# Stacking the high and low parts of the 64 sample tokens in one 128-column stationary operand

## The chip, the core and the metric

The kernel runs on one core of one Trainium2 chip. The metric is the device time of one execution in microseconds (us); the number for a kernel is the median of its runs. Five engines work side by side, each through its own list of instructions in order: TensorE (PE, matrix products; PEld is its load of the stationary operand), VectorE (DVE), ScalarE (ACT), GpSimd (POOL) and SyncE (SP), which here only starts DMA transfers. They wait for each other through semaphores.

## What is computed

The reference is one inference step of a hybrid layer, for 2048 prompt tokens and 64 sample tokens of another stream. Cut to what matters:

```python
h = rms_norm(x, norm_g)                      # x: prompt (2048, 1024), sample (64, 1024)
proj = h @ w_in                              # (1024, 6656), then split in ten column groups
o_hg = hgrn2_chunkwise(silu(hg_q), k_in, hg_i, log_f, s_hg)       # 8 heads, carries a state
o_rt = retention_chunkwise(rope(rt_q), rope(rt_k), rt_v, s_rt)    # 4 heads, carries a state
o_xa = softmax(xa_q @ mem_k.T / sqrt(128)) @ mem_v                # 4 heads, 256 memory tokens
mixed = concat([norm(o_hg) * silu(hg_gate), norm(o_rt) * silu(rt_gate), o_xa * silu(xa_gate)])
y = rms_norm(x + mixed @ w_out, final_norm_g)                     # w_out: (2048, 1024)
```

The operands are float32. To keep the accuracy, the kernel splits every operand of a large product into a high part (rounded to the type that TensorE reads in one pass) and a low part (the rest), and sums three products: high x high, high x low, low x high.

## The kernel before

The 2112 tokens are worked on in two groups (GROUPS): tiles of 512 and 512 tokens, then of 512, 256 and 320. The last tile holds 256 prompt tokens and, as its last subchunk, the 64 sample tokens (DEC). For each group the normed, transposed tokens stand in SBUF as a high and a low buffer (ha, hb). Then come, in this order: the retention gates, the values of the retention (RV, `v_group`), its queries and keys (RQ, `retention`), and for each half of the HGRN heads their values (HI, `v_group` again) and four heads; then the memory attention; at the end, over all tokens, the output projection.

Most projections are column-major (`gemm_col`, L243): weights are stationary and tokens move. RV, RQ and the two HI are token-major (`gemm_tok`, L273): 128 tokens, or the 64 sample tokens, are the stationary operand, and 512 weight columns move past them. One such product has 8 slices of the 1024 inputs, and for each three matmuls (L278): high tokens x high weights, low tokens x high weights, high tokens x low weights. That is 24 matmuls. The output projection (`y_half`, L1091) takes one block of 128 tokens (the last block is the 64 sample tokens) and one half of the 1024 output columns: 16 slices of 128, three matmuls each, so 48 matmuls for a half.

What sets the order: PE's and SP's lists stand as the code is written. Around the big products, tails (transposes, scores, state updates) are put into PE's list by a planner (`task`, `poll`): each has a due time in PE's planned time, which `pe()` counts up with every matmul. ACT, DVE and POOL are ordered by a scheduler by priority. Weights come through three staging buffers (wst), are split by ACT (the cast, L240) and DVE (the difference, L241) into six pairs (whi, wlo); a pair comes free where `w_rel` stands (L282: after every second slice of the last token-major product of a stage), which starts the split of a later slab and then its refill by DMA (L141). In the retention each subchunk loads a table for the rotation (cs, L593, three buffers), rotates (L600 to L606, DVE), then its tail transposes r (L618), copies it (L622 to L626, ACT), forms scores (L635), outputs (L651, L655), norms (L675 to L683) and transposes back (L691). `slot()` gives scratch tiles from one pool of 16.

The output projection loads a block of the mixed rows (mst, 512 KB in two transfers), splits it (L240, L241), adds the product to x (L1103), squares with a sum (L1104), scales (L1119) and stores. The x block stands in abuf or xq by turns. `y_load` of the next block is issued in the middle of a block.

Of the kernel before, what the change touches and what calls it, by code (L numbers as in the profile page):

```python
# [63 lines left out]
def layer_kernel(ctx: ExitStack, tc: tile.TileContext, io: dict):  # L64
# [115 lines left out]
    def allow_alloc(tag):  # L180
        return [t.rearrange("p k n -> p (k n)") for t in h_tile(tag, 512 if tag == "a" else 576)]
# [41 lines left out]
    def small(n, tag):  # L223
        return sm.tile([P, n], F32, tag=tag, name=tag)
# [47 lines left out]

    def gemm_tok(ws, ht, o, L, rel=False):  # L273
        ps = acc()
        n = 0
        for kk in range(KT):
            w = wt[ws[kk // 2]]
            for a, b in ((0, 0), (0, 1), (1, 0)):  # L278
                T.matmul(ps[0:L, :], ht[b][:, kk, o:o + L], w[a][:, kk % 2, :], start=(n == 0), stop=(n == 23))  # L279
                n += 1  # L280
                pe(512 / 2400.0)
            if rel and kk % 2 == 1:  # L282
                w_rel()
            if kk < KT - 1:
                poll()
        return ps
# [72 lines left out]
    def h_split(ht, sts, bcs, nt):  # L359
        for kk in range(KT + 1):  # L360
            if kk < KT:
                st = sts[kk]
                V.scalar_tensor_tensor(out=st, in0=st, scalar=ng[:, kk:kk + 1], in1=bcs[:, 0:nt], op0=ALU.mult, op1=ALU.mult)
                S.copy(ht[0][:, kk, 0:nt], st)
            if kk:
                V.tensor_tensor(out=ht[1][:, kk - 1, 0:nt], in0=sts[kk - 1], in1=ht[0][:, kk - 1, 0:nt].bitcast(F32), op=ALU.subtract)  # L366
            yield kk
# [17 lines left out]
    def h_tile(tag, n):  # L385
        return [hpool.tile([P, KT, n], F32R, tag=f"{tag}{i}", name=f"h{tag}{i}") for i in range(2)]
# [201 lines left out]
    def retention(ws, ht, tok0, nt, vt, R, dtab, last_tile):  # L588
        for c, (o, L) in enumerate(subchunks(tok0, nt)):
            t = tok0 + o  # L590
            ti = t // 128
            ct_ = sm.tile([P, 96], F32, tag="cs", name="cs", bufs=3)
# [4 lines left out]
            ps = gemm_tok(ws, ht, o, L, last_tile and o + L == nt)  # L597
            r = slot()
# [204 lines left out]
    def prep_tile(gi, i, gap, sts=None, tot=None, delay=0):  # L803
        tok0, nt = GROUPS[gi][i]
        if i == 0:
            ht = h_tile("a", 512)
        elif i == 1:
            hmap["b"] = h_tile("b", 576)
            ht = [b_[:, :, 0:nt] for b_ in hmap["b"]]
        else:  # L810
            ht = [b_[:, :, 256:256 + nt] for b_ in hmap["b"]]
        done = [False]
        g = prep_h(ht, [L for _, L in subchunks(tok0, nt)], tok0 // 128, io["xT"][:, tok0:tok0 + nt], sts, tot, delay, gap, done)
        task(None, g, 0)
        hmap[gi, i] = ht
        hdone[gi, i] = done
# [16 lines left out]
    mh = h_tile("b", 576)  # L833
# [65 lines left out]
    h0 = h_tile("a", 512)  # L899
# [57 lines left out]

    def y_load(o, raw):
        L = 128 if o < SEQ else DEC
        src = io["x_prompt"][0, o:o + L] if o < SEQ else io["x_sample"][0]  # L960
        if (o // 128) % 2:
# [5 lines left out]
        for mv in raw:  # L967
            hi, lo = slot(F32R), slot(F32R)
            hv = hi.rearrange("p (k l) -> p k l", k=4)[:, :, 0:L]
            lv = lo.rearrange("p (k l) -> p k l", k=4)[:, :, 0:L]  # L970
            split(hv, lv, mv)
            m.append((hv, lv))
# [4 lines left out]
    for gi, tiles in enumerate(GROUPS):  # L977
        hts = [h_get(gi, 0)]

        def v_group(c0):  # L980
            ws = w_get(4)
            out = []
            for (tok0, nt), ht in zip(tiles, hts):
                vs = []
                for o, L in subchunks(tok0, nt):
                    ps = gemm_tok(ws, ht, o, L, tok0 + o + L == tiles[-1][0] + tiles[-1][1])
                    v = vpool.tile([P, 512], F32, tag="v", name="v")
                    S.copy(v[0:L], ps[0:L])
# [102 lines left out]
    def y_half(mx, x, ss, L, half):  # L1091
        ps = acc()
        n = 0
        for kk in range(16):
            w = wo[half, kk]
            m = mx[kk // 4]
            for a, b in ((0, 0), (1, 0), (0, 1)):
                T.matmul(ps[0:L], m[a][:, kk % 4], w[b], start=(n == 0), stop=(n == 47))  # L1098
# [3 lines left out]
        xs = x[half][0:L]  # L1102
        V.tensor_tensor(out=xs, in0=xs, in1=ps[0:L], op=ALU.add)  # L1103
        S.activation(ps[0:L], xs, AF.Square, accum_out=ss[0:L, half:half + 1])  # L1104

    for o in range(0, NTOK, 128):
# [5 lines left out]
        if o + 128 < NTOK:  # L1112
            nxt = y_load(o + 128, mix_fetch(o + 128, 128 if o + 128 < SEQ else DEC, False))
# [106 lines left out]
```

## Time and profile before

| | |
|---|---|
| median of 3 runs | 1980.01 us (1978.01 to 1980.36) |
| span of the profiled execution, first to last instruction | 1976.5 us; the page gives no time of this execution beside its span |
| PE busy | 1936.0 us, 98% of the span |
| DVE, ACT, POOL busy | 1045.4 us (53%), 583.5 us (30%), 161.4 us (8%) |
| mean granted TensorE clock | 0.993 of the full clock |
| DMA | 153.20 MB, 25.3% of the 16 engines' span on the main queue |
| chain that ended last | PE 86%, DVE 6%, DMA 2%, ACT 2% |

The page has the busy time of each engine, the span in 40 slices, the chain of work that ended last and the costliest groups. Below it, the trace can be asked for the instructions in order of time (the timeline), for one line's instructions, and for the waits.

### The profile page before, as it was taken

How to read it: one execution, taken by the hardware profiler on the slowest of the kernel's cores; microseconds unless marked ns; L12 is line 12 of the kernel's file. 1: busy time of each engine (PE TensorE's matmuls, PEld its weight loads, DVE VectorE, ACT ScalarE, POOL GpSimd, SP SyncE). 2: the span in 40 equal slices, each digit the busy share in tenths (PEclk: the TensorE clock that was granted, in tenths of full speed). 3: DMA queues.
4: the chain of work that ended last, by engine and by line, in shares of the span. 5: the costliest groups of instructions: out<-in, count | busy, mean ns of one | idle time of the engine just before them, and what ended most of it. 6: DMA issues, size and time to landing. Idle time of an engine off the chain costs nothing.

```text
span 1976.5 us, 28228 instructions
## 1 busy us (share of the span) xinstructions
PE 1936.0 (98%) x10970; PEld 1624.4 (82%) x10970; DVE 1045.4 (53%) x2505; ACT 583.5 (30%) x1414; POOL 161.4 (8%) x363
## 2 busy tenths in 40 slices
PE   8899999999999999999999999999999999999998
PEld 7788788888888887978788888888889878888885
DVE  6716637762767557417637774477765632222221
ACT  5522223322233434312322332233333521111110
POOL 3100101000100100000101111021100000000000
PEclk8999999999999999999999999999999999999999
DMA  7422311211112524321311111111122442332221
GB/s 249 139 70 66 87 50 48 59 54 49 44 43 59 155 64 137 92 60 53 86 43 48 48 48 48 43 49 48 59 73 73 125 132 85 99 114 86 86 86 43
DMA packets 116742, 153.20 MB, mean 78 GB/s; under 512 B 13313, under 2 KB 79233, under 8 KB 116609
## 3 DMA queue, kind: packets, MB, share of 16 engines
q1 hardware_dynamic: 116608, 151.41, 25.3%
q8 instruction: 86, 1.41, 0.3%
q14 instruction: 48, 0.39, 0.1%
HBM read 117.69 MB, written 33.69 MB: 77 GB/s over the span
## 4 chain that ended last, share of the span: by engine, by line
PE 86%; DVE 6%; DMA 2%; ACT 2%; issue 1%; POOL 1%; SPq 0%; DVEq 0%; POOLq 0%; ACTq 0%
PE acc L249 38%; PE acc L1098 19%; PE acc L279 16%; PE scb L514 2%; PE ob L523 2%; PE ob L555 1%; PE ob L558 1%; PE acc L783 1%; PE ob L739 1%; DVE wlo L241 1%; PE acc L264 1%; PE tr L507 1%; PE tr L574 1%; POOL rs L237 1%; PE tr L761 1%
## 5 line engine op out<-in xcount | busy, mean ns | idle before, releaser
L249 PE MATMUL acc<-hb,whi 128*128 128x320 f32 (+2 forms) x1728 | 414.5, 330 | 0.4 <-DVE hb L366 0.4
L249 PE MATMUL acc<-ha,whi 128*128 128x512 f32 x1120 | 353.3, 397 | 0.0
L249 PEld LDWEIGHTS acc<-hb,whi 128*128 128x128 f32 x1728 | 289.5, 189 | 24.7 <-issue 4.4
L241 DVE TENSOR_TENSOR wlo<-wst,whi 128x1024 fp32r<-128x1024 f32 x118 | 146.5, 1246 | 277.0 <-ACT whi L240 276.0
L249 PE MATMUL acc<-hb,wlo 128*128 128x320 f32 (+2 forms) x864 | 281.5, 326 | 0.0
L249 PEld LDWEIGHTS acc<-ha,whi 128*128 128x128 f32 x1120 | 203.8, 188 | 42.8 <-issue 2.4
L249 PE MATMUL acc<-ha,wlo 128*128 128x512 f32 x560 | 219.1, 391 | 0.0
L240 ACT CAST whi<-wst 128x1024 fp32r<-128x1024 f32 x118 | 123.6, 1050 | 223.2 <-PE acc L249 171.7
L279 PE MATMUL acc<-whi,hb 128*128 128x512 f32 (+1 forms) x576 | 180.0, 394 | 0.0
L249 PEld LDWEIGHTS acc<-hb,wlo 128*128 128x128 f32 x864 | 163.1, 189 | 11.2
L279 PE MATMUL acc<-whi,ha 128*128 128x512 f32 x512 | 161.0, 396 | 0.0
L1098 PE MATMUL acc<-whi,s 128*128 128x512 f32 (+1 forms) x408 | 128.9, 397 | 1.3 <-ACT s L240 1.0
L249 PEld LDWEIGHTS acc<-ha,wlo 128*128 128x128 f32 x560 | 105.1, 188 | 23.0
L279 PEld LDWEIGHTS acc<-whi,hb 128*128 128x128 f32 (+1 forms) x576 | 103.0, 182 | 25.1 <-issue 1.2
L279 PE MATMUL acc<-wlo,hb 128*128 128x512 f32 (+1 forms) x288 | 112.3, 390 | 0.0
L279 PEld LDWEIGHTS acc<-whi,ha 128*128 128x128 f32 x512 | 93.8, 188 | 19.7 <-issue 1.2
L1098 PE MATMUL acc<-hb,s 128*128 128x512 f32 (+1 forms) x408 | 100.3, 402 | 0.0
L279 PE MATMUL acc<-wlo,ha 128*128 128x512 f32 x256 | 100.0, 391 | 0.0
L1098 PE MATMUL acc<-ha,s 128*128 128x512 f32 (+1 forms) x408 | 98.1, 395 | 0.0
L1098 PEld LDWEIGHTS acc<-hb,s 128*128 128x128 f32 (+1 forms) x408 | 77.0, 189 | 20.3
L241 DVE TENSOR_TENSOR s<-mst,s 128x512 fp32r<-128x512 f32 (+1 forms) x64 | 40.3, 672 | 99.2 <-ACT s L240 99.2
L1098 PEld LDWEIGHTS acc<-whi,s 128*128 128x128 f32 (+1 forms) x408 | 75.0, 184 | 21.5 <-ACT s L240 1.3
(223 smaller groups left out, 2888.0 us busy)
## 6 DMA issues: line engine op xcount, KB each, us to landing
wst<-w_in_t SPq DMA_DIRECT2D x104, 512.0 KB, 4.0
mixT<-s SPq DMA_DIRECT2D x64, 256.0 KB, 4.0
mst<-mixT SPq DMA_DIRECT2D x30, 512.0 KB, 5.9
wst<-w_out_t SPq DMA_DIRECT2D x16, 512.0 KB, 4.0
s<-mixT SPq DMA_DIRECT2D x16, 256.0 KB, 3.0
s<-x_prompt SPq DMA_DIRECT2D x16, 256.0 KB, 4.7
xq<-x_prompt SPq DMA_DIRECT2D x16, 256.0 KB, 4.9
abuf<-x_prompt SPq DMA_DIRECT2D x16, 256.0 KB, 5.8
```

The lines of the kernel that those rows point to most:

```text
L237: G.tensor_tensor(out=out, in0=out, in1=nhalf[0:out.shape[0], 0:n], op=ALU.pow)
L240: S.copy(hi, src)
L241: V.tensor_tensor(out=lo, in0=src, in1=hi.bitcast(F32), op=ALU.subtract)
L249: T.matmul(ps[:, 0:nt], w[a][:, kk, :], ht[b][:, kk, 0:nt], start=(n == 0), stop=(n == 23))
L264: T.matmul(ps[:, 0:nt], w[a][:, kk, :], ht[b][:, kk, 0:nt], start=(kk == 0 and a + b == 0), stop=(kk == KT - 1 and a == 1))
L279: T.matmul(ps[0:L, :], ht[b][:, kk, o:o + L], w[a][:, kk % 2, :], start=(n == 0), stop=(n == 23))
L507: T.transpose(trk[0:L, c * 128:(c + 1) * 128], kch[:, c * 128:c * 128 + L], ident)
L514: T.matmul(scb[32 * e:32 * e + 32, c * 128 + 32 * e:c * 128 + L], K[:, c * 128 + 32 * e:c * 128 + 32 * e + 32], Qe[:, c, E_OFF[e]:E_OFF[e] ...
L523: T.matmul(db[:, c * 128:(c + 1) * 128], kT[0:L, c * 128:(c + 1) * 128], vt[c][0:L], start=True, stop=True)
L555: T.matmul(ob[0:L, c * 128:(c + 1) * 128], A[0:L, c * 128:c * 128 + L], vt[c][0:L], start=True, stop=first)
L558: T.matmul(ob[0:L, c * 128:(c + 1) * 128], qst[:, c * 128:c * 128 + L], st[c][0], start=False, stop=True)
L1098: T.matmul(ps[0:L], m[a][:, kk % 4], w[b], start=(n == 0), stop=(n == 47))
```

## The change

For the 64 sample tokens alone, the high and the low part are put side by side: 64 columns of high, 64 of low, in one stationary operand of 128 columns. One matmul with the high weights then gives high x high in output rows 0 to 63 and low x high in rows 64 to 127; a second one, with the low weights, adds high x low (and low x low in the lower rows). A `fold` adds the two halves of the result: ACT copies rows 64 to 127 to a scratch tile, DVE adds that to rows 0 to 63.

- Token-major: the high buffer hb0 grows from 576 to 640 columns a slice, and one more ACT copy, run once when the last tile is prepared, writes the low part of the sample tokens behind the high part (`hstk`). The sample's product is 16 matmuls in place of 24, four times (RV, RQ, HI twice). For RV and HI the fold writes v in place of ACT's copy; for RQ it writes a scratch tile pf, from which the rotation then reads.
- Output projection: the sample's mixed rows are split straight into the stacked form; a half has 32 matmuls in place of 48, and ACT's copy and a second DVE add follow it. The sample block is moved from last place to the last but one; the last block is now the 128 tokens from 1920.
- The rotation tables (cs) have two buffers in place of three, and so have Te and rT of the HGRN heads.

```diff
     def small(n, tag):
-        return sm.tile([P, n], F32, tag=tag, name=tag)
+        return sm.tile([P, n], F32, tag=tag, name=tag, bufs=2 if n == 32 else 3)
...
+    def fold(dst, ps):
+        t = slot()
+        S.copy(t[0:DEC], ps[DEC:P])
+        V.tensor_tensor(out=dst, in0=ps[0:DEC], in1=t[0:DEC], op=ALU.add)
+
     def gemm_tok(ws, ht, o, L, rel=False):
...
             w = wt[ws[kk // 2]]
+            if L == DEC:
+                for a in range(2):
+                    T.matmul(ps, hstk[0][:, kk, :], w[a][:, kk % 2, :], start=(n == 0), stop=(n == 15))
+                    n += 1
+                    pe(512 / 2400.0)
+                if rel and kk % 2 == 1:
+                    w_rel()
+                if kk < KT - 1:
+                    poll()
+                continue
...
+            if kk == KT and nt == 320:
+                S.copy(hstk[0][:, :, DEC:P], ht[1][:, :, 256:320].bitcast(F32))
             yield kk
...
-        return [hpool.tile([P, KT, n], F32R, tag=f"{tag}{i}", name=f"h{tag}{i}") for i in range(2)]
+    def h_tile(tag):
+        return [hpool.tile([P, KT, n], F32R, tag=f"{tag}{i}", name=f"h{tag}{i}") for i, n in enumerate({"a": (512, 512), "b": (640, 576)}[tag])]
...
-            ct_ = sm.tile([P, 96], F32, tag="cs", name="cs", bufs=3)
+            ct_ = sm.tile([P, 96], F32, tag="cs", name="cs", bufs=2)
...
             ps = gemm_tok(ws, ht, o, L, last_tile and o + L == nt)
+            if L == DEC:
+                pf = slot()
+                fold(pf[0:L], ps)
+                ps = pf
...
+    order = list(range(0, SEQ - P, P)) + [SEQ, SEQ - P]
+
     def y_load(o, raw):
...
-            hi, lo = slot(F32R), slot(F32R)
...
+            hi = slot(F32R).rearrange("p (k l) -> p k l", k=4)
+            if L == DEC:
+                split(hi[:, :, 0:L], hi[:, :, L:P], mv)
+                m.append((hi, hi))
+                continue
...
-                    S.copy(v[0:L], ps[0:L])
+                    if L == DEC:
+                        fold(v[0:L], ps)
+                    else:
+                        S.copy(v, ps)
...
-            for a, b in ((0, 0), (1, 0), (0, 1)):
-                T.matmul(ps[0:L], m[a][:, kk % 4], w[b], start=(n == 0), stop=(n == 47))
+            terms = ((0, 0), (1, 0), (0, 1)) if L == P else ((0, 0), (0, 1))
+            for a, b in terms:
+                T.matmul(ps, m[a][:, kk % 4], w[b], start=(n == 0), stop=(n == 16 * len(terms) - 1))
...
         xs = x[half][0:L]
+        if L == DEC:
+            t = slot()
+            S.copy(t[0:L], ps[L:P])
+            V.tensor_tensor(out=xs, in0=xs, in1=t[0:L], op=ALU.add)
         V.tensor_tensor(out=xs, in0=xs, in1=ps[0:L], op=ALU.add)
...
-    for o in range(0, NTOK, 128):
+    for i_, o in enumerate(order):
```

How the lists of the engines change is seen at three places. In the rows, s is a scratch tile, acc a result of PE, tr a transposed result, scb scores, cs the rotation table, mst the loaded mixed rows; a row is line, operation, output<-inputs and shape. Line numbers of the changed kernel are shifted: its L706 is L683 of the kernel before, L623 to L629 are L600 to L606, L651 is L628, L662 is L639, L716 is L693, L649 is L626, L703 is L680, L1140 and L1141 are L1103 and L1104.

DVE at the end of the retention of the second group, before:

```order
L241 TENSOR_TENSOR wlo<-wst,whi 128x1024 x2
L683 TENSOR_TENSOR s<-s,rs_8081 128x512
L628 TENSOR_TENSOR s<-tr,cst 128x256
L600 TENSOR_TENSOR s<-acc,cs 64x512
L693 TENSOR_TENSOR s<-s,tr 128x512
L604 TENSOR_TENSOR s<-acc,cs 64x8x32
L605 TENSOR_TENSOR s<-acc,cs 64x8x32
L606 TENSOR_TENSOR s<-s 64x512
L608 TENSOR_TENSOR s<-s,cst 64x256
```

The same stretch of DVE's list in the changed kernel:

```order
L241 TENSOR_TENSOR wlo<-wst,whi 128x1024 x2
L706 TENSOR_TENSOR s<-s,rs_8082 128x512
L276 TENSOR_TENSOR s<-acc,s 64x512
L623 TENSOR_TENSOR s<-s,cs 64x512
L627 TENSOR_TENSOR s<-s,cs 64x8x32
L628 TENSOR_TENSOR s<-s,cs 64x8x32
L629 TENSOR_TENSOR s<-s 64x512
L631 TENSOR_TENSOR s<-s,cst 64x256
L651 TENSOR_TENSOR s<-tr,cst 128x256
L662 TENSOR_TENSOR s<-scb,s 128x512
L716 TENSOR_TENSOR s<-s,tr 128x512
```

The fold's add (L276) and the sample's rotation now stand ahead of the two passes L651 and L716 that belong to the subchunks before.

ACT at the same place, before:

```order
L240 CAST whi<-wst 128x1024 x3
L622 COPY q2b_139<-tr 64x2x128
L623 COPY q2b_139<-tr 64x2x128
L240 CAST whi<-wst 128x1024
L680 ACTIVATE s,ss_8075<-s 128x128 x4
L626 COPY s<-tr 128x256
```

ACT there in the changed kernel (q2b takes the two copies of the transposed queries, ss a sum of squares):

```order
L240 CAST whi<-wst 128x1024 x4
L645 COPY q2b_139<-tr 64x2x128
L646 COPY q2b_139<-tr 64x2x128
L703 ACTIVATE s,ss_8076<-s 128x128 x4
L275 COPY s<-acc 64x512
L649 COPY s<-tr 128x256
```

The fourth cast of weights has moved ahead of the query copies, and the fold's copy (L275) stands ahead of the key copy L649, for which the scores on PE wait.

ACT at the end of the output projection, before:

```order
L1104 ACTIVATE acc,ss_16599<-xq 128x512 x2
L240 CAST s<-mst 128x4x64 x4
L1104 ACTIVATE acc,ss_16732<-abuf_109 128x512
L1104 ACTIVATE acc,ss_16732<-abuf_111 128x512
L1104 ACTIVATE acc,ss_16866<-xq 64x512 x2
```

And in the changed kernel:

```order
L240 CAST s<-mst 128x4x64 x4
L1141 ACTIVATE acc,ss_16578<-xq 128x512 x2
L1138 COPY s<-acc 64x512
L240 CAST s<-mst 128x512 x3
L1141 ACTIVATE acc,ss_16707<-abuf_109 64x512
L240 CAST s<-mst 128x512
L1138 COPY s<-acc 64x512
L1141 ACTIVATE acc,ss_16707<-abuf_111 64x512
L1141 ACTIVATE acc,ss_16815<-xq 128x512 x2
```

The sample's casts (128x4x64) now come one block earlier, and the four full casts of the last block stand between the two copies of the sample block.

## Rows read from the trace of the kernel before

**Rows 1.** Page, part 1: busy us (share of the span) and instructions of each engine.

```profile
PE 1936.0 (98%) x10970; PEld 1624.4 (82%) x10970; DVE 1045.4 (53%) x2505; ACT 583.5 (30%) x1414; POOL 161.4 (8%) x363
```

**Rows 2.** Timeline of PE, second HI: start us, us, engine, line, instruction.

```profile
1243.96 0.61 PE L279 MATMUL acc<-whi,hb 128*128 128x512 f32 x2
...
1250.08 0.63 PE L279 MATMUL acc<-whi,hb 128*64 128x512 f32 x2
...
1255.60 0.61 PE L249 MATMUL acc<-ha,whi 128*128 128x512 f32 x2
```

**Rows 3.** Timeline of DVE, last two blocks of the output projection.

```profile
1935.38 0.69 DVE L1103 TENSOR_TENSOR abuf<-abuf,acc 128x512 f32<-128x512 f32 x1 [0.38 <-PE acc L1098]
1946.59 0.69 DVE L1103 TENSOR_TENSOR abuf<-abuf,acc 128x512 f32<-128x512 f32 x1 [10.52 <-PE acc L1098]
...
1957.68 0.68 DVE L1103 TENSOR_TENSOR xq<-xq,acc 64x512 f32<-64x512 f32 x1 [7.04 <-PE acc L1098]
...
1968.78 0.68 DVE L1103 TENSOR_TENSOR xq<-xq,acc 64x512 f32<-64x512 f32 x1 [10.42 <-PE acc L1098]
```

**Rows 4.** View of L279: ns min/median/max, first and last start, forms.

```profile
L279 PEld LDWEIGHTS acc<-whi,hb x576: 133/188/192, 120.7 to 1254.9; 128*128 128x128 f32 x171, 128*64 128x64 f32 x21
```

**Rows 5.** Timelines around the end of RV, second group, engine by engine.

```profile
868.72 0.63 PE L279 MATMUL acc<-whi,hb 128*64 128x512 f32 x2
...
886.80 0.63 PE L618 MATMUL tr<-cst,s 128*128 128x128 f32 x4 [0.16 <-DVE s L606]
...
870.06 1.05 ACT L240 CAST whi<-wst 128x1024 fp32r<-128x1024 f32 x1 [0.56 <-PE acc L279]
...
874.43 0.58 ACT L988 COPY v<-acc 64x512 f32<-64x512 f32 x1 [0.56 <-PE acc L279]
876.04 1.05 ACT L240 CAST whi<-wst 128x1024 fp32r<-128x1024 f32 x1 [1.03 <-DMA wst<-w_in_t]
...
877.12 1.23 DVE L241 TENSOR_TENSOR wlo<-wst,whi 128x1024 fp32r<-128x1024 f32 x1 [1.99 <-ACT whi L240]
884.57 0.69 DVE L600 TENSOR_TENSOR s<-acc,cs 128x512 f32<-128x512 f32 x1 [6.22 <-DMA cs<-rope]
...
881.68 4.60 SPq L593 DMA_DIRECT2D cs<-rope  x4
```

**Rows 6.** Timelines at the end of the retention, second group, engine by engine.

```profile
946.46 0.63 PE L279 MATMUL acc<-whi,hb 128*64 128x512 f32 x2
...
958.88 1.13 PE L635 MATMUL scb<-q2b,s 128*128 128x256 f32 x4 [2.04 <-ACT s L626]
...
964.65 0.46 PE L618 MATMUL tr<-cst,s 64*128 64x64 f32 x4
...
958.45 0.37 ACT L626 COPY s<-tr 128x256 f32<-128x256 f32 x1
...
960.51 0.69 DVE L683 TENSOR_TENSOR s<-s,rs 128x512 f32<-128x512 f32 x1 [1.18 <-POOL rs L237]
...
963.42 0.68 DVE L606 TENSOR_TENSOR s<-s 64x512 f32<-64x512 f32 x1
```

**Rows 7.** Timelines of SP and DVE: a rotation table in the retention.

```profile
915.62 0.55 SPq L593 DMA_DIRECT2D cs<-rope  x1
923.20 0.36 SPq L127 DMA_DIRECT2D mixT<-s  x1
...
919.83 0.41 DVE L605 TENSOR_TENSOR s<-acc,cs 128x256 f32<-128x256 f32 x1
```

**Rows 8.** Timelines of SP and ACT: loads of the last blocks.

```profile
1906.26 1.20 SPq L954 DMA_DIRECT2D mst<-mixT  x2
...
1928.65 1.20 SPq L954 DMA_DIRECT2D mst<-mixT  x2
...
1912.89 1.14 ACT L240 CAST s<-mst 128x512 fp32r<-128x512 f32 x2 [0.65 <-DMA mst<-mixT]
```

**Rows 9.** DMA view: KB each, median us from issue to landing.

```profile
o_yp<-xq SPq DMA_DIRECT2D x16, 256.0 KB, 2.3
```

More of the change, by code (lines that the diff above doesn't have):

```diff
@@ L180, in allow_alloc @@
     def allow_alloc(tag):
-        return [t.rearrange("p k n -> p (k n)") for t in h_tile(tag, 512 if tag == "a" else 576)]
+        return [t.rearrange("p k n -> p (k n)") for t in h_tile(tag)]
     wnext = [0]
@@ L383, in prep_h @@
         done[0] = True
-    def h_tile(tag, n):
-        return [hpool.tile([P, KT, n], F32R, tag=f"{tag}{i}", name=f"h{tag}{i}") for i in range(2)]
+    def h_tile(tag):
+        return [hpool.tile([P, KT, n], F32R, tag=f"{tag}{i}", name=f"h{tag}{i}") for i, n in enumerate({"a": (512, 512), "b": (640, 576)}[tag])]
+    hstk = []
     def x_chunks(t0_, nt):
@@ L805, in prep_tile @@
         if i == 0:
-            ht = h_tile("a", 512)
+            ht = h_tile("a")
         elif i == 1:
-            hmap["b"] = h_tile("b", 576)
+            hmap["b"] = h_tile("b")
             ht = [b_[:, :, 0:nt] for b_ in hmap["b"]]
@@ L811, in prep_tile @@
             ht = [b_[:, :, 256:256 + nt] for b_ in hmap["b"]]
+            hstk.append(hmap["b"][0][:, :, 512:640])
         done = [False]
@@ L832, in layer_kernel @@
     mg = cols[:, 36:44]
-    mh = h_tile("b", 576)
+    mh = h_tile("b")
     wsrc += [(io["w_mk_t"][h], 128, "w") for h in range(4)]
@@ L898, in layer_kernel @@
     mps = [acc(), scb]
-    h0 = h_tile("a", 512)
+    h0 = h_tile("a")
     hmap[0, 0], hdone[0, 0] = h0, [True]
@@ L960, in y_load @@
         src = io["x_prompt"][0, o:o + L] if o < SEQ else io["x_sample"][0]
-        if (o // 128) % 2:
+        if order.index(o) % 2:
             x = a_buf
@@ L967, in y_load @@
         for mv in raw:
-            hi, lo = slot(F32R), slot(F32R)
[L969 to L972, printed above, removed]
+            hi = slot(F32R).rearrange("p (k l) -> p k l", k=4)
[3 more added lines that the diff above has]
+                continue
+            lo = slot(F32R).rearrange("p (k l) -> p k l", k=4)
+            split(hi, lo, mv)
+            m.append((hi, lo))
         for i in range(2):
@@ L1111, in layer_kernel @@
         y_half(mx, x, ss, L, 0)
-        if o + 128 < NTOK:
-            nxt = y_load(o + 128, mix_fetch(o + 128, 128 if o + 128 < SEQ else DEC, False))
+        if o != order[-1]:
+            o2 = order[i_ + 1]
+            nxt = y_load(o2, mix_fetch(o2, P if o2 < SEQ else DEC, False))
         y_half(mx, x, ss, L, 1)
```

## The prediction

> **What bounds the kernel now.** I read the busy shares first, then the order in time around each place that the change touches. PE is busy for 98% of the span; DVE and ACT stand at 53% and 30% [rows 1]. So time comes out of this kernel mainly by taking columns off PE. But a share is a mean: at a few places PE waits for a chain through ACT, DVE and SP, and there fewer matmuls only make PE wait longer. So the question at each of the changed places is: which comes last, the matmuls or that chain?
>
> A matmul row lasts 0.39 us, but they overlap, so its price is the distance between starts. For 128 stationary columns it is (1250.08 - 1243.96)/27 = 0.2267 us, for the 64 columns of the sample (1255.60 - 1250.08)/24 = 0.230 us [rows 2]. A half-empty stationary operand thus costs as much as a full one, and that is what the change uses: filling the other 64 columns adds nothing to the start-to-start time.
>
> **The change part by part.** It removes 64 matmuls: 8 in each of four token-major products, 16 in each of the two halves of the sample's output block. On PE alone that is:
>
> - token-major: 24 x 0.230 = 5.52 us before, 16 x 0.2267 = 3.63 us after, so 1.89 us each;
> - output projection: a half of the sample block takes 11.09 to 11.10 us (from one DVE add to the next), a half of a 128-token block 11.21 us, so 0.2335 us a matmul [rows 3]. A half becomes 32 x 0.2335 = 7.47 us, and both save 22.19 - 14.95 = 7.24 us.
>
> All paid out, that is 4 x 1.89 + 7.24 = 14.8 us. Now place by place.
>
> *HI, twice.* After the sample's product PE goes on with a column-major product of 24 matmuls, 5.4 us, before anybody needs a new vector result. The fold costs one copy (0.58 us, which the old copy cost too) [rows 5] and one DVE add of 64 rows (0.68 us) [rows 3], with DVE waiting for casts there. Nothing on PE waits for v at once. I take the full 1.89 us each, 3.79 us. If the cover is gone, the weight chain of RV, next, is what would show.
>
> *RV, second group.* Here the product is followed by the retention, whose first PE work that needs DVE is the transposition at 886.80; PE comes there just in time, it waits 0.16 us [rows 5]. What DVE was late for is a table: its pass at 884.57 had waited 6.22 us for the DMA of cs. That DMA was issued at 881.68, behind four weight transfers, the last of which needs the staging buffer that the difference at 877.12 frees; that waits for the cast at 876.04, that for a weight DMA, and that one for the first cast at 870.06, which starts when PE has read the second weight slice [rows 5]. This chain starts two matmuls earlier (the third matmul is the last that reads the high slab, not the fifth): 2 x 0.23 = 0.46 us. The fold's add falls into DVE's gap of 1.99 us before 877.12. So PE comes 1.89 us earlier, finds the table 0.46 us earlier, and waits 1.4 us more. Gain 0.46 us; bounds 0.3 and 1.89.
>
> *RQ, the sample subchunk.* In the trace PE stands at 958.88 for 2.04 us, waiting for ACT's key copy at 958.45; the next places wait for DVE, which works almost without a gap: its pass at 960.51 waited for POOL, and the sample's r is ready at 963.42 + 0.68 = 964.10 [rows 6]. PE then takes the transposition at 964.65. None of this starts earlier because the sample has fewer matmuls, as the rows ahead of it on DVE and ACT belong to older subchunks. And two things are put into it: the fold's copy (0.58 us) ahead of the key copy, and the fold's add (0.68 us) ahead of the rotation; two DVE passes of about that sum move behind. So r is ready near 964.1 again. By the new list PE has then done 18 matmuls of HI, not 21, and goes on about 0.45 us earlier than 964.65: 3 x 0.2267 - 0.45 = 0.2 us behind, and gets some of it back because the sample is interleaved with one switch less. I take 0.0 us; bounds -0.6 (both fold steps in line half uncovered) and 1.89.
>
> *Output projection.* The sample block is now followed by a full block, whose load must be done in 14.95 us rather than 22.4. In the trace the load issued at 1906.26 has its last casts end at 1912.89 + 1.14 = 1914.03, 7.8 us later; the next one is issued at 1928.65 [rows 8], so a full load there is split by 1936.4, plus some 1.3 us for the fold's copies and adds between the casts. The block before the sample ends its products at 1935.38 - 11.21 = 1924.2 [rows 3], the sample block then at 1924.2 + 14.95 = 1939.1. That is 1.4 us to spare for the last of the four parts, and the first part is what is needed first. So 7.24 us are paid out. If the load came later, PE would wait for it one for one.
>
> *The end.* After the last matmul come the same six steps as before, over 128 rows rather than 64: the add takes 0.69 rather than 0.68 us [rows 3], so 0.05 us over all. The last store is 256 KB rather than 128; such a store lands in 2.3 us [rows 9], so at most 1.15 us if time went with bytes. I take 0.1.
>
> *Two buffers rather than three.* A rotation table can now be loaded only when DVE has read the one two subchunks back. One load, at 915.62, would be held until 919.83 + 0.41 = 920.24; SP's next work is at 923.20 [rows 7]. So nothing is late. Te and rT are written and read by DVE alone, in the same order as before: 0. The copy into hstk runs once, ACT having 70% free [rows 1]: 0.
>
> Sum: 3.79 + 0.46 + 0.0 + 7.24 - 0.1 = 11.4 us. The span is 1976.5 us, so 1965.1; the median of the runs lies 3.5 us above the span, and I keep that distance: 1980.0 - 11.4 = 1968.6 us.
>
> *A rule against it.* A load of 64 columns takes 133 ns in the trace, one of 128 columns 188 ns, 55 ns more [rows 4], and yet the 128-column matmuls follow each other no slower [rows 2]: the load lies under the matmul before. The Trainium skill, page "TensorE: Matmul & The Clock Gate", says in "LDWEIGHTS (loading the stationary operand)" that the load goes by columns, and in "The mechanism" (Part 3) that it overlaps with running matmuls only where the row group differs. The rows agree with the first (its rate gives, as an estimate, 53 ns for 64 columns) and speak against the second.
>
> **The rivals.**
>
> 1. *All of it is paid out.* The chains at RV and RQ move up with the matmuls. For it: ACT and DVE have half their time free. Against it: the 6.22 us at the table and the 2.04 us at the scores. Gain 14.8 - 0.1 = 14.7, time 1965.3.
> 2. *HI pays out no more than RV.* Both HI free their weight slabs in the same way, and the chain of cast, difference, DMA, cast would then end after the product that follows. Gain 11.4 - 2 x (1.89 - 0.46) = 8.5, time 1971.5. Against it: there is no table behind those weights.
> 3. *The wider loads are not hidden.* 128 matmuls have the new form, 55 ns each: 7.0 us, of the gain 4.4 are left, time 1975.6. The starts speak against it [rows 2].
> 4. *Slower: SP is held by the two table buffers.* If a held table lets the gate rows or the next table come late, PE stands for one subchunk, 24 x 0.2267 = 5.4 us. Three such stalls among the 17 subchunks cost 16.3 us, time 1980.0 + 4.9 = 1984.9; from 2.1 stalls on, the kernel is slower. Against it: the one hold that I find ends 3 us before SP has other work [rows 7].
>
> **How the numbers follow.** Chances: forecast 0.62, rival 1 0.15, rival 2 0.12, rival 3 0.03, rival 4 0.04; the last 0.04 are for a loss that I don't see which eats most of the gain. The forecast's own terms reach from 1965 (RV or RQ pays out) to some 1970 (RQ -0.6, the last store 1.15). With rivals 1 and 2 and about 1 us of scatter of a median (the three runs span 2.4 us), the range is 1964.0 to 1973.0; rivals 3 and 4 and the rest lie outside. A measurement can tell 0.2%, 4.0 us, from no change: faster is below 1976.0. Forecast and rivals 1 to 3 are faster, with rival 3 at the edge: 0.91. Within 0.2%: 0.05. Slower: 0.04.
>
> **What would show it.** In the profile after: 64 fewer matmuls of 512 columns; starts 0.227 us apart in the sample's products and 0.2335 in its output block; about 7.5 us between its two DVE adds. HI's next product starts 1.9 us earlier after the sample's first matmul. A new wait of some 1.8 us on PE at the retention's first transposition, for the rotation (which waits for the table), and at the retention's end a wait for the key copy of 3 us or more, with a further one, 1 to 2 us, at the sample's transposition. No wait of PE in the last block. The prediction is wrong if those waits are missing (rival 1), if PE waits after HI (rival 2), if the starts are further apart (rival 3), or if a table lands after its product has ended (rival 4).

## The result, and the profile after

The changed kernel takes 1966.28 us (median of 4 runs, 1962.78 to 1968.01), the kernel before in the same series 1980.13 us (4 runs, 1978.01 to 1980.36): a ratio of 0.9938, 95% interval 0.9923 to 0.9953, so 9 to 15 us less. The forecast was 1968.6 with a range of 1964.0 to 1973.0. In later series the same two kernels gave 1966.35 (6 runs) and 1978.1 (all 57 runs of before taken together, 1972.22 to 1982.49). The times of both scatter by 8 to 10 us; where that comes from is a part of what follows.

The first two lines of the page of after, which answer to [rows 1]: 64 matmuls are gone, PE is 98% busy as before.

```profile
span 1966.2 us, 28106 instructions
PE 1924.1 (98%) x10906; PEld 1624.0 (83%) x10906; DVE 1049.2 (53%) x2511; ACT 584.6 (30%) x1418; POOL 163.9 (8%) x363
```

**HI.** Timeline of PE in the second HI, to be set against [rows 2]: the first stacked matmul of the sample, and the first matmul of the product that follows.

```profile
1249.13 0.39 PE L285 MATMUL acc<-whi,hb 128*128 128x512 f32 x1
...
1252.76 0.62 PE L249 MATMUL acc<-ha,whi 128*128 128x512 f32 x2
```

The sample takes 3.63 us where it took 5.52; 16 starts are 0.227 us apart, and nothing waits behind them. The first HI shows the same (3.62).

**RV.** Timelines of PE, DVE and SP of after, as in [rows 5] (start, duration, engine, line, operation; in brackets the idle time before it and what ended it).

```profile
869.47 0.39 PE L285 MATMUL acc<-whi,hb 128*128 128x512 f32 x1
...
886.66 0.66 PE L641 MATMUL tr<-cst,s 128*128 128x128 f32 x4 [1.17 <-DVE s L629]
...
884.53 0.69 DVE L623 TENSOR_TENSOR s<-acc,cs 128x512 f32<-128x512 f32 x1 [5.81 <-DMA cs<-rope]
...
882.04 6.64 SPq L612 DMA_DIRECT2D cs<-rope  x4
```

From the sample's first matmul to the retention's first transposition it is 17.19 us, before 18.08. The wait that was 0.16 us is 1.17 us, and behind it is again the table: DVE stood 5.81 us for its DMA.

**RQ.** The same place as [rows 6], on PE, ACT and DVE.

```profile
959.06 2.03 PE L658 MATMUL scb<-q2b,s 128*128 128x256 f32 x4 [2.67 <-ACT s L649]
961.02 1.12 PE L668 MATMUL ob<-v,s 128*64 128x128 f32 x8
...
964.45 0.46 PE L641 MATMUL tr<-cst,s 64*128 64x64 f32 x4 [0.81 <-DVE s L651]
...
958.04 0.57 ACT L275 COPY s<-acc 64x512 f32<-64x512 f32 x1
958.63 0.37 ACT L649 COPY s<-tr 128x256 f32<-128x256 f32 x1
...
960.83 0.68 DVE L276 TENSOR_TENSOR s<-acc,s 64x512 f32<-64x512 f32 x1
...
962.93 0.68 DVE L629 TENSOR_TENSOR s<-s 64x512 f32<-64x512 f32 x1
...
963.99 0.41 DVE L651 TENSOR_TENSOR s<-tr,cst 128x256 f32<-128x256 f32 x1
```

The fold's copy (958.04) stands ahead of the key copy, the fold's add (960.83) ahead of the rotation, as the order said. PE waits 2.67 us for the key copy (2.04 before), and 0.81 us more ahead of the sample's transposition. Before, PE had a second wait here too, of 0.76 us, ahead of another transposition:

```profile
961.35 0.63 PE L691 MATMUL tr<-cst,s 128*128 128x128 f32 x4 [0.76 <-DVE s L683]
```

So the two waits grew from 2.80 to 3.48 us. What releases the sample's transposition is not its own rotation, whose last pass (L629) ends at 963.61, but L651, which ends at 964.40. The transposition writes into one of two PSUM buffers (`trp`), and L651 has to read that buffer first; L651 is one of the two passes that the new order puts behind the sample's rotation.

Something else is new: the scores, 1.13 us before, take 2.03 us. Two views by stretches tell why (columns: PE busy and its instructions, granted clock, DMA share, GB/s); after, then before:

```profile
953.00:959.00 6.00, 3.39 (x17) 1.00 0.44 129
959.00:964.40 5.40, 4.58 (x19) 0.68 1.02 339
964.40:968.00 3.60, 3.55 (x18) 1.00 0.63 183
```

```profile
956.00:966.00 10.00, 7.20 (x40) 1.00 0.86 252
```

After the longer wait the granted clock fell from the full level (2.4 GHz) to the half (1.2 GHz) for most of 5.4 us; in the profile of before it stayed at 1.00. Whether that fall costs anything here is settled by `early_table` below.

**Output projection.** DVE's adds in the last blocks of after, which answer to [rows 3]. L1139 adds the low half of the sample block, L1140 the rest; the last two rows are the last full block.

```profile
1921.69 0.69 DVE L1140 TENSOR_TENSOR xq<-xq,acc 128x512 f32<-128x512 f32 x1 [10.51 <-PE acc L1131]
...
1929.77 0.68 DVE L1139 TENSOR_TENSOR abuf<-abuf,s 64x512 f32<-64x512 f32 x1 [4.03 <-ACT s L1138]
...
1937.23 0.68 DVE L1139 TENSOR_TENSOR abuf<-abuf,s 64x512 f32<-64x512 f32 x1 [1.15 <-ACT s L1138]
...
1947.82 0.69 DVE L1140 TENSOR_TENSOR xq<-xq,acc 128x512 f32<-128x512 f32 x1 [5.79 <-PE acc L1131]
1959.02 0.69 DVE L1140 TENSOR_TENSOR xq<-xq,acc 128x512 f32<-128x512 f32 x1 [10.51 <-PE acc L1131]
```

From the last add ahead of the sample block to the first of the last full block it is 26.13 us: 11.20 for that half and 14.93 for the sample's two halves (forecast 14.95). PE doesn't wait in the last block. From the last add ahead of the last two blocks to the last add it is 1959.02 - 1921.69 = 37.33 us; before it was 1968.78 [rows 3] less the start of this add, 44.60 us, so 7.27 us are gained:

```profile
1924.18 0.69 DVE L1103 TENSOR_TENSOR xq<-xq,acc 128x512 f32<-128x512 f32 x1 [8.74 <-PE acc L1098]
```

From the last add to the end of the span it is 7.2 us, before 7.7 us.

### The profile page after: what moved, and what is told of

Its sections match the earlier page's. It is cut to its first block, busy times and chain, and to the rows that moved or that the text cites. A ratio compares the mean times of both kernels' runs of the same rounds, so it can differ in the third digit from the quotient of the medians.

```text
span 1966.2 us, 28106 instructions
## 1 busy us (share of the span) xinstructions
PE 1924.1 (98%) x10906; PEld 1624.0 (83%) x10906; DVE 1049.2 (53%) x2511; ACT 584.6 (30%) x1418; POOL 163.9 (8%) x363
## 4 chain that ended last, share of the span: by engine, by line
PE 87%; DVE 6%; DMA 3%; ACT 2%; issue 1%; POOL 1%; SPq 0%; DVEq 0%; POOLq 0%; ACTq 0%
PE acc L249 39%; PE acc L1131 19%; PE acc L294 15%; PE scb L533 2%; PE ob L542 2%; PE ob L574 2%; PE ob L577 1%; PE acc L806 1%; PE ob L762 1%; DVE wlo L241 1%; PE acc L264 1%; PE tr L593 1%; PE tr L526 1%; PE tr L784 1%; DMA wst<-w_mv_t 1%
## 5 line engine op out<-in xcount | busy, mean ns | idle before, releaser
L294 PE MATMUL acc<-whi,hb 128*128 128x512 f32 x512 | 160.1, 394 | 0.0
L1131 PE MATMUL acc<-whi,s 128*128 128x512 f32 x396 | 125.9, 396 | 1.3 <-ACT s L240 1.0
L294 PEld LDWEIGHTS acc<-whi,hb 128*128 128x128 f32 x512 | 94.5, 188 | 19.9 <-issue 1.2
L294 PE MATMUL acc<-wlo,hb 128*128 128x512 f32 x256 | 99.8, 390 | 0.0
L1131 PE MATMUL acc<-hb,s 128*128 128x512 f32 x400 | 98.5, 403 | 0.0
L1131 PE MATMUL acc<-ha,s 128*128 128x512 f32 x400 | 96.4, 396 | 0.0
L1131 PEld LDWEIGHTS acc<-hb,s 128*128 128x128 f32 x400 | 76.9, 192 | 18.7
L1131 PEld LDWEIGHTS acc<-whi,s 128*128 128x128 f32 x396 | 74.3, 188 | 19.6 <-ACT s L240 1.3
```

Of the source, the lines that this page charges most:

```text
L1131: T.matmul(ps, m[a][:, kk % 4], w[b], start=(n == 0), stop=(n == 16 * len(terms) - 1))
```

## Experiments

Medians move by several microseconds from series to series, so each kernel is also measured by its stages, in its own trace. Three of them carry the argument: **RV**, from the sample's first RV matmul to the retention's first transposition; **RQ**, from that transposition to the sample's first matmul in the first HI; **clock**, the granted clock between 956 and 966 us. The later sections refer to this table, whose numbers are differences of starts on PE, in us.

```
kernel        median    ratio to before [95%]     RV     RQ      clock  wait at scores
before        1978.1    1                         18.08  123.90  1.00   2.04
two_tables    1978.96   1.0005 [0.9994, 1.0016]   17.86  124.69  0.83   2.06
hi_only       1975.07   0.9983 [0.9973, 0.9994]   17.76  124.70  0.83   2.02
out_only      1972.59   0.9974 [0.9963, 0.9985]   18.01  124.71  0.83   2.06
rv_rq_only    1977.92   1.0005 [0.9995, 1.0015]   17.29  124.64  0.83   2.68
no_rq         1966.07   0.9944 [0.9924, 0.9963]   17.39  123.77  1.00   1.76
after         1966.28   0.9938 [0.9923, 0.9953]   17.19  124.65  0.83   2.67
after_again   1966.35   0.9942 [0.9925, 0.9959]   17.21  124.65  0.83   2.67
one_table     1966.66   0.9937 [0.9919, 0.9955]   17.24  124.54  0.83   2.68
early_table   1966.45   0.9942 [0.9925, 0.9958]   15.87  126.02  0.88   2.68
filled        1961.93   0.9921 [0.9902, 0.9939]   17.01  120.50  1.00   1.00
both          1960.89   0.9913 [0.9895, 0.9931]   15.87  120.44  1.00   1.00
both_no_rq    1959.10   0.9904 [0.9889, 0.9919]   15.87  120.99  1.00   none
both2         1958.80   0.9903 [0.9885, 0.9921]   15.87  119.17  1.00   none
```

### The change in parts

Each part alone: a flag decides where `gemm_tok` uses the stacked operand. Of the changed kernel this is HI alone (the output projection goes back to 48 matmuls a half and to the old order of blocks); `c0 == RV` with the fold kept in RQ gives the second, `False` with the new output projection the third.

```diff
-    def gemm_tok(ws, ht, o, L, rel=False):
+    def gemm_tok(ws, ht, o, L, rel=False, stk=True):
...
-            if L == DEC:
+            if L == DEC and stk:
...
+                    stk = c0 != RV
-                    ps = gemm_tok(ws, ht, o, L, tok0 + o + L == tiles[-1][0] + tiles[-1][1])
+                    ps = gemm_tok(ws, ht, o, L, tok0 + o + L == tiles[-1][0] + tiles[-1][1], stk)
```

> Only the two HI products of the sample use the stacked operand; RV, RQ and the output projection run as in the kernel before. Theory (forecast): both products pay in full, 16 starts instead of 24, so each stage from the sample's product to the next landmark is 1.9 us shorter and the kernel gains 3.8 us (about 1976.3 us beside 1980.1). Rival (HI pays no more than RV, because a weight chain then comes last): 0.5 us each, 0.9 us together, about 1979.2 us, and a new wait of PE of some 1.4 us after each of the two products.

1975.07 us, ratio 0.9983: 3.4 us less by the ratio (1.2 to 5.3). In the trace both products take 3.62 and 3.63 us instead of 5.52, with no wait behind them: 3.79 us, paid in full. The rival (HI pays no more than RV) falls.

> Only the sample's RV and RQ products use the stacked operand; both HI products and the output projection run as before. Theory: the matmuls removed at these two places are nearly worthless, since PE then waits longer for the rotation table (RV) and for the key copy and the sample's rotation (RQ): from the profile of the changed kernel RV +0.9 us and RQ -0.6 us, so 0.3 us in all, about 1979.8 us, with a wait of 1.2 us at the retention's first transposition and of 2.7 us at the scores ahead of the sample's transposition. Rival (both pay in full, the loss in the profile being chance): 3.8 us, about 1976.3 us.

1977.92 us, ratio 1.0005 (1.0 us less to 3.0 us more): these 16 matmuls are worth nothing that a median can show, and the rival's 3.8 us lie outside. The waits are there as expected, 1.25 us at the first transposition and 2.68 us at the scores. The table above says more than the sum: RV gains some 0.7 us, RQ is where it was in those unstacked kernels that lost the clock there.

> Only the output projection is stacked, with its new order of blocks; all four token-major products run as before. Theory: the sample block's two halves take 14.9 us instead of 22.2, no wait in the last block, and the end after the last matmul is no longer than before: 7.2 to 7.8 us gained, about 1972.5 us. Rival (the last full block's load is late, or the larger last store costs): PE waits up to 3 us in the last block or the end is up to 1.2 us longer, 1974 to 1976 us.

1972.59 us, ratio 0.9974: 5.1 us less (3.0 to 7.3), under the expected 7.2 to 7.8 in the median. The trace shows the expected time: the stretch from the last add ahead of the sample block to the last add is 37.34 us, in after 37.33, and the end is short (7.19 us). What the median lacks, some 2 us, can for the most part be the clock: its mean over the 12 runs is 0.9914, over the 29 runs of before 0.9925. In the runs of before 0.01 of clock goes with 14 us (a line through all 53 with a recorded clock), so this difference would be some 1.5 us, an estimate. So the stage was right; why the clock fell more often in these runs is open.

### RQ without the stacked operand

```diff
-            ps = gemm_tok(ws, ht, o, L, last_tile and o + L == nt)
-            if L == DEC:
-                pf = slot()
-                fold(pf[0:L], ps)
-                ps = pf
+            ps = gemm_tok(ws, ht, o, L, last_tile and o + L == nt, False)
```

> The changed kernel with only the sample's RQ product put back to 24 matmuls and no fold there. Theory: RQ's stacked form costs 0.6 us, because the fold's copy stands ahead of the key copy on ACT and the fold's add ahead of the rotation on DVE, and because PE's clock falls after the longer wait at the scores. Without it the wait there is 2.0 us again, the granted clock stays at 1.00 between 956 and 966 us, and the kernel is 0.6 us faster than the changed one, with fewer runs that lose to the clock. Rival (the saved matmuls are paid out at RQ too): 1.9 us slower than the changed kernel.

1966.07 us, which can't be told from the changed kernel. In this trace the clock stayed at 1.00 and RQ is 123.77 us, 0.88 less than in after and as good as before: so far the expectation came true. But three other kernels with 24 matmuls in RQ lost the clock (two_tables, hi_only, out_only), and theirs is 124.69 to 124.71. The view by stretches of hi_only and of no_rq:

```profile
956.00:966.00 10.00, 7.98 (x35) 0.83 0.79 240
```

```profile
956.00:966.00 10.00, 7.48 (x42) 1.00 0.81 244
```

So it depends on the execution what the unfilled stacked RQ (124.54 to 124.65 us, but for early_table) is worth: 0.05 us against an unstacked one that lost its clock, and 0.8 us less than nothing against one that kept it (123.77 and 123.90, two profiles of five). The expectation's other reason, that the stacked RQ loses time because its clock falls, is wrong, as the next but one section shows.

### The changed kernel again

> The changed kernel once more, unaltered, for its median over more runs and a second trace. Theory: by the stages of the profiles the change takes 0.9 us at RV, -0.6 at RQ, 1.9 twice at HI, 7.3 between the adds of the output projection and 0.5 at the end, 11.9 us in all; what the runs show beyond or below that (13.9 us between the first medians, 10.3 us between the two profiled spans) is the clock, which falls after waits of PE of about 2 us at five places in some executions and not in others, at about 1.7 us each. So the median stands 11 to 13 us below that of the kernel before in the same call, with single runs up to 4 us to either side. Rival (the changed kernel itself has more such falls): less than 10 us.

1966.35 us, before in the same series 1976.57 (11 runs); the ratio is 0.9942, 11.5 us (8 to 15), the difference of the medians 10.2. The first lies inside the expected 11 to 13 us, the second below; the interval doesn't exclude the rival. The stages repeat to 0.02 us, the span doesn't (1963.7 and 1966.2), and it differs in where the clock fell: the second HI starts at 1249.13 and 1249.20, and the 2.5 us come behind it, where after lost its clock near 1594 us (1.00 granted in after_again, 0.77 in after between 1590 and 1605) and after_again near 1455 us.

### The rotation table loaded early

```diff
+            ct0 = rope_load(tiles[0][0], P)
             vts = v_group(RV)
...
-            ct_ = sm.tile([P, 96], F32, tag="cs", name="cs", bufs=2)
-            dma(ct_[0:L], io["rope"][ti, 0:L])
+            ct_ = first_ct if first_ct is not None and c == 0 else rope_load(t, L)
```

> The changed kernel with the first rotation table of a group loaded ahead of RV's products instead of behind the weight transfers. Theory: the wait at the retention's first transposition, 1.17 us, is the table's alone, so it goes away and the stage from the sample's RV product to that transposition is 1.2 us shorter (16.0 rather than 17.2 us); 1.2 us off the whole kernel. Rival: the rotation is held by something else that comes just as late (DVE's differences for the weights, the fold), the wait stays above 0.8 us and nothing is gained.

The wait is gone; PE of early_table around the place of [rows 5], with no brackets at the transposition:

```profile
870.15 0.39 PE L285 MATMUL acc<-whi,hb 128*128 128x512 f32 x1
...
886.02 0.60 PE L644 MATMUL tr<-cst,s 128*128 128x128 f32 x4
```

RV is 15.87 us, 1.3 less than in after, and 15.87 again in every other kernel with this edit. With hi_only's 17.76, an unstacked RV that finds PE without a wait, that makes 1.89 us: the whole price of the 8 matmuls, so it was the table alone that held RV back. Yet the median didn't move (1966.45): in this profile RQ took 126.02 us. PE waited 2.68 us at the scores and 2.06 us at the sample's transposition, and the clock fell after the second, where nothing covers it (0.64 between 964.4 and 968 us):

```profile
958.33 1.13 PE L661 MATMUL scb<-q2b,s 128*128 128x256 f32 x4 [2.68 <-ACT s L652]
...
963.72 0.69 PE L644 MATMUL tr<-cst,s 64*128 64x64 f32 x4 [2.06 <-DVE s L654]
```

This trace also tells what the fall at the scores in after cost: nothing. Here the scores ran at full clock (1.13 us), and yet the sample's transposition came 77.70 us after the retention's first one (963.72 - 886.02), in after 77.79 (964.45 - 886.66). PE only waited longer for DVE, 2.06 rather than 0.81 us. Behind the transposition, after needs 46.86 us to HI's sample product; both2, with 24 fewer matmuls left and no fall, needs 41.39. The difference is 5.47, and 24 matmuls at 0.2267 us are 5.44. So a stacked RQ with an unbroken clock would take about 124.6 us as well, an estimate from these rows.

### The waits at RQ filled

Three delays of the planner are raised at the end of the retention. With them 36 matmuls of HI, not 18, stand ahead of the sample's transposition; the last three hunks lead from there to both2, with 42. In both_no_rq, with 33, the three delays are raised by 2.0, 2 and 3.0.

```diff
-        yield D_RT1
+        yield D_RT1 + (2.5 if t == SEQ - P else 0.0)
...
-        yield D_RT3
+        yield D_RT3 + (2 if t == SEQ - 2 * P else 0.0)
...
-            task("rt", retention_tail(...), D_RT0)
+            task("rt", retention_tail(...), D_RT0 + (4 if L == DEC else 0.0))
...
-        yield D_RT1 + (2.5 if t == SEQ - P else 0.0)
+        yield D_RT1 + (3.5 if t == SEQ - P else 0.0)
...
-        yield D_RT3 + (2 if t == SEQ - 2 * P else 0.0)
+        yield D_RT3 + (3.5 if t == SEQ - 2 * P else 0.0)
...
-            task("rt", retention_tail(...), D_RT0 + (4 if L == DEC else 0.0))
+            task("rt", retention_tail(...), D_RT0 + (5 if L == DEC else 0.0))
```

> The changed kernel with three delays of the planner raised for the last prompt subchunk's scores, for the last step of the subchunk before it and for the sample's transposition, so that 36 matmuls of HI stand ahead of the sample's transposition instead of 18. Theory: in RQ the chain through DVE and ACT sets when the scores and the sample's transposition can run (key copy at 959.0 us, transposition at 964.4 us), and PE only has too little to do meanwhile; so both run at the same times as now, 18 matmuls of HI, 4.1 us, are done in the waits, and the clock doesn't fall there: 3.5 to 4.1 us faster than the changed kernel. Rival (the chain is itself held by PE's order): the transposition comes later by what is put ahead of it, and nothing is gained.

1961.93 us, 4.4 less than the changed kernel by the medians, and in the trace RQ is 124.65 - 120.50 = 4.15 us shorter, 18 matmuls at 0.23 us. PE of filled: the scores wait 1.00 us, the sample's transposition not at all. It stands 1.10 us later than in after, but this kernel came 1.14 us later to the retention's first transposition already (887.80 and 886.66).

```profile
961.21 1.13 PE L658 MATMUL scb<-q2b,s 128*128 128x256 f32 x4 [1.00 <-ACT s L649]
...
965.55 0.46 PE L641 MATMUL tr<-cst,s 64*128 64x64 f32 x4
```

So the chain through ACT and DVE sets the times there, and PE had only lacked work.

> The changed kernel with the early table and the filled waits together. Theory: the two places are independent, so 1.2 and 3.5 to 4.1 us add up, 4.7 to 5.3 us below the changed kernel and 16 to 18 us below the kernel before. Rival (the place at RQ takes back what RV gains, since its chain doesn't start earlier): 3.5 to 4.1 us only.

1960.89 us, 5.5 less than the changed kernel; RV 15.87, RQ 120.44, in sum 5.55 less than in after_again. That is a little over the expected 4.7 to 5.3: the two places are independent and add up.

> The kernel with the early table and the filled waits, with the planner's delays raised a little more, so that 30 matmuls of HI rather than 24 stand ahead of the last full scores and 42 rather than 36 ahead of the sample's transposition. Theory: the wait of 1.0 us that is left at those scores is filled too; 6 more matmuls are 1.36 us, of which 1.0 is gained. Rival (the chain of DVE has become late by now): the transposition is pushed back by the 0.4 us or more that don't fit and the gain is under 0.5 us.

1958.80 us; RQ 119.17, 1.27 less than both (expected 1.0). PE no longer waits at the scores, nor at the transposition, and the clock stays up:

```profile
956.00:966.00 10.00, 9.98 (x64) 1.00 0.80 262
```

It beats both kernels of the case, ratio to before 0.9903 [0.9885, 0.9921].

> The kernel with the early table and the filled waits, but with the sample's RQ product put back to 24 matmuls and no fold there; 33 matmuls of HI stand ahead of the sample's transposition. Theory: what the stacked RQ product is worth depends on what PE can do meanwhile. With the waits filled, the matmuls saved at RQ are replaced by HI's, so that stacking now gains 0.7 us or more, where it lost 0.7 us without the filling: this kernel is 0.7 to 1.9 us slower than the one with both. Rival (the fold is what costs at RQ, whatever PE does): it is 0.6 us faster.

The medians (1959.10 and 1958.80) can't tell it from both2, the stages can: with PE waiting nowhere in RQ, 24 matmuls take 120.99 us and 16 take 119.17. Stacking RQ is now worth 1.82 us of its 1.89; without the filling it was worth 0.05 at best and cost 0.8 at worst.

### The table buffers

```diff
-            ct_ = sm.tile([P, 96], F32, tag="cs", name="cs", bufs=2)
+            ct_ = sm.tile([P, 96], F32, tag="cs", name="cs", bufs=1)
```

> The changed kernel with one buffer for the rotation tables instead of two, so that every load of a table has to wait on SP for the rotation of the subchunk before. It prices the prediction's slower rival. Theory (forecast): the table is then issued when the rotation before has ended, some 3 us into a product of 5.4 us, and lands 2.5 us later, so a rotation comes about a microsecond late and PE seldom notices: 0 to 3 us slower than the changed kernel. Rival 4: weight and gate transfers queue behind the held table, and PE stands for most of a product at several subchunks: 5 us for each such place, 16 us for three, and the kernel is slower than before.

1966.66 us, the changed kernel's time. The trace shows loads that are held, and nobody who minds; SP and DVE of one_table:

```profile
882.29 13.60 SPq L612 DMA_DIRECT2D cs<-rope  x4
...
888.06 0.69 DVE L623 TENSOR_TENSOR s<-acc,cs 128x512 f32<-128x512 f32 x1 [0.73 <-DMA cs<-rope]
```

Four table loads take 13.60 us on SP instead of 6.64, a rotation starts 0.73 us late, and RV and RQ are those of after. The other kernel is the one before with `bufs=2` in place of 3.

> The kernel before with two buffers for the rotation tables instead of three and nothing else changed. Theory: no wait of PE changes, the stages of the retention stay within 0.1 us, the time is that of the kernel before. Rival 4: at least one subchunk's table comes late, and PE stands for up to 5.4 us there.

1978.96 us, ratio 1.0005 [0.9994, 1.0016]: no price. The stages didn't stay within 0.1 us of before, as was expected: its RQ is 0.8 us longer, but its clock fell there, and it equals hi_only and out_only; its RV is 0.2 us shorter.

## Why the prediction was right, and where not

- **HI, 3.79 us: right.** 5.52 to 3.62 and 3.63 us, no wait behind. This also settles the wider loads (rival 3): 16 matmuls with 128 stationary columns, all loaded anew, in 3.63 us.
- **RV, 0.46 us: the chain right, the size low.** The table left SP 12.57 us after the sample's first matmul, before 12.96: 0.39 us earlier, where 0.46 was worked out. The rotation that waits for it then began 2.49 us later, not 2.89, which nobody had forecast. By the table of kernels, unstacked RV (18.08, 17.86, 17.76, 18.01) less stacked (17.01 to 17.39) is 0.7 us. The step that failed was to take the landing time of one transfer as fixed; it scatters from kernel to kernel, and how much of the gain is luck isn't shown.
- **RQ, 0.0 us: the waits right, the size wrong in this pair (-0.75), and the reason overlooked.** The waits came (2.67 us at the scores, where "3 us or more" was said, and 0.81 us at the sample, where "1 to 2" was). The step that failed is that PE goes on 0.45 us earlier at the sample's transposition. Counted from the retention's first transposition it came at 77.79 us, before at 77.85: 0.06 us earlier, with 18 matmuls of HI done rather than 21, so 0.62 us behind where the forecast had 0.2; the last 0.1 us isn't accounted for. The sample's r was indeed ready earlier (963.61, before 964.10), but the transposition waited for L651 until 964.40. The fall of the clock in after is not the cause. It is rather the unstacked RQ that loses by a fall: there PE comes to the transposition without a wait, and so 0.8 us later.
- **Output projection, 7.24 us: right.** The stretch to the last add is 37.33 us in place of 44.60: 7.27 us. The two adds of the sample block are 7.46 us apart (1929.77 and 1937.23), and the load was in time.
- **The end, -0.1 us: wrong sign.** It is 0.5 us shorter. Some 0.2 us of it is the last store, which now has 128 rows and lands no later; the section on the hardware has the rows. The rest isn't explained.
- **Two buffers, 0: right.** The held load that was put at 920.24 us was issued at 920.22, and even one buffer costs nothing. Rival 4 falls.
- **The base: wrong by 1.7 us.** The forecast put the median 3.5 us above the span and kept that distance. In the later runs each time stands 1.73 to 1.86 us above its own span (hi_only 1971.5 and 1973.26, after 1966.2 and 1968.01), so the profiled execution of before took about 1976.5 + 1.8 = 1978.3 us, and the forecast had set its span beside the median of other executions. 1978.3 - 11.4 is 1966.9.

By stages the gain is 3.79 + 0.7 + 7.27 + 0.5 = 12.3 us without RQ, and 11.5 to 12.3 with it (-0.8 to 0.05); the medians of all runs give 1978.1 - 1966.35 = 11.75, the forecast had 11.4. That its sum came so near is in part luck: RV and the end were put too low by 0.2 and 0.6 us, RQ too high by up to 0.8. The measured 1966.28 lies nearer to rival 1 (1965.3) than to the forecast, but not for rival 1's reason: the waits that it denied are there, and taking them away (early_table, both2) brings out nearly the microseconds that it had counted.

The two profiled spans differ by 10.3 us. The stages of this pair make 3.79 + 0.89 - 0.75 + 7.27 + 0.5 = 11.7; the rest is lost between the stages, 0.75 us of it ahead of RV (868.72 before, 869.47 after), where after lost its clock near 661 us and before near 40 us.

## What to carry to other kernels

Fewer matmuls pay where PE goes on to work that waits for nobody (HI, the output projection), and turn into a wait where a transfer or a chain of ACT and DVE comes last (RV, RQ); the same 8 matmuls of RQ were worth 0.05 us or less with that wait and 1.82 us once other matmuls had filled it. So when such a saving is lost, don't undo it: load the late table earlier, or move independent matmuls into the gap. Look also at what a new step pushes back on its engine: L651, moved behind the rotation, held the buffer that PE needed next. And compare stages of like kernels, with the granted clock beside them, when the medians scatter by more than the effect.

## What the runs showed of the hardware

**A wait of about 2 us may halve the clock, or not.** At the scores of RQ, PE waited 1.76 to 2.68 us in ten profiles; the clock fell behind that wait or the next in eight, and in none of the four profiles where the wait was 1.00 us or none. All five with 2.67 or 2.68 us lost it, three of five with 1.76 to 2.06; that the longer wait makes it likelier is suggested by this, not shown. What a fall costs depends on what comes last behind it: nothing up to the sample's transposition in after, where DVE came last anyway, 0.8 us in the unstacked RQ, 1.4 us in early_table, where it came behind the wait. Near 766 us the same wait, 2.29 to 2.32 us, was followed by a fall in ten of fourteen. After and before near 661 us, after equal last waits of 2.22 us:

```profile
655.00:675.00 20.00, 17.43 (x81) 0.91 0.27 92
```

```profile
655.00:675.00 20.00, 17.78 (x97) 1.00 0.36 123
```

That is most of the scatter: a line through the times of before against the mean clock takes up 73% of their variance. Of 53 runs of before with a recorded clock, the six with a mean of 0.995 span 1970.4 to 1971.9 us, the nine with 0.989 or 0.990 span 1976.8 to 1980.1. What decides in a given execution stays open.

**A store of 64 rows isn't faster than one of 128.** From the issue-by-size view of after (KB each, median us to landing):

```profile
o_yp<-xq SPq DMA_DIRECT2D x18, 256.0 KB, 2.1
...
o_ys<-abuf SPq DMA_DIRECT2D x2, 128.0 KB, 2.3
```

Twice the bytes land in 2.1 rather than 2.3 us; in the trace of before the medians are 2.3 us for both [rows 9]. At the end of the kernel, where only the two halves of the last block are stored, the last store lands 2.28 us after its issue in before (64 rows) and 2.07 us in after (128 rows), 0.2 us. The last multiplications start 5.1 us before the end in three kernels that store the sample last (before, hi_only, two_tables) and 4.6 us where a full block is stored last. But in rv_rq_only, which stores the sample last too, it is 4.8 us, so the remaining 0.3 us isn't the size of the store; it lies behind the landing, and its cause is open.

**Loads of the stationary operand.** The Trainium skill, page "TensorE: Matmul & The Clock Gate", says in "The mechanism" (Part 3) that such a load overlaps with running matmuls only where the row group differs; the same section also lets a load be pulled ahead into a background weight buffer. The stacked loads and their matmuls use all 128 rows, and 16 of them take 3.63 us, 0.227 each; by the rule of the row group each of the 128 would have added its 188 ns [rows 4]. The trace disagrees with that rule; whether it is the background buffer that hides the loads, no run here shows.
